# Seam of a hybrid layer kernel: feed forward's input sums reordered by product, first weight strip requested early, last block's residual rows written by accumulating transfers

## Chip, core and metric

One core of a Trainium2 chip runs the whole kernel. The metric is device time in microseconds (us) of one execution. All data are float32; TensorE works on pairs of float32r tiles ("hi" and "lo" parts), so that one product of full precision is three matmuls.

## Reference, cut to what matters

The layer works on `x` of 2048 tokens by 1024 channels. `chunked_gated_delta_rule`, the convolutions and the norms of the first half are left out here.

```python
h = adaln(x, g_norm_mix, shift_m, scale_m)
p = h @ w_in                       # 1024 -> 3592
...                                # convolutions, gated delta rule: ya, yb
y = concatenate([ya, yb]) @ w_out  # 1024 -> 1024
x = x + gate_m * y

h = adaln(x, g_norm_ffn, shift_f, scale_f)
gt, up = split(h @ w_gate_up, 2)   # 1024 -> 2 x 2816
x = x + gate_f * ((silu(gt) * up) @ w_down)
return adaln(x, g_norm_final, shift_o, scale_o)
```

## The kernel before, in words

The tokens are cut into 4 blocks of 512. The first half of the program (the mixing) takes them one after another: projections with `w_in`, convolutions, delta rule, and at the end of each block the out-projection with `w_out`. The second half (feed forward) first does gate and up with SiLU for 22 strips of 128 hidden channels, for two halves of the tokens, then the product with `w_down`. The seam is where the last block's out-projection ends and the first strip begins.

**Out-projection.** For block 3 it has two groups, one for each half of the output columns. A group is 4 weight pieces (`KPS`, order 0, 2, 3, 1) by 4 row tiles of 128 tokens, 24 matmuls a piece, and holds four PSUM banks of the pool `pd`, which has four. At its end each bank is read by VectorE (L1345, times `gate_m`) into a `cv` buffer (four of them); the old rows of `x` have been loaded into `cb` (L1343, two buffers), are added (L1346, by VectorE in the last block and by GpSimd in the others), and the sum is stored to the DRAM rows `x1d` (L1347). The second group can only start in a bank when VectorE has read it.

**Feed forward's sums.** Gate and up use a fast scheme of seven products in place of eight: `A11`, `A12`, `S2`, `S1`, `S3`, `S4`, `A22` on the token side (`SUMS`), and `B11`, `B21`, `T2`, `T1`, `T3`, `B22`, `T4` on the weight side. The token side is made from the normed, transposed input of blocks 0 and 1, which lies in DRAM as `xTd` (8 tiles of 128 x 512 per block). `first_sums` goes over `k` in 0 to 3; for each it loads four tiles, scales them on ScalarE (`load_scaled`, L603), and then makes all six sums' parts of this `k`: VectorE adds and subtracts (L623 to L629), and each result is split into hi (ScalarE cast, L598) and lo (VectorE subtract, L599) by `split_k`. So no sum is whole before the last `k`. `last_sum` makes `A22` after that. `run` walks one strip through the seven products in the order of `SUMS`.

**Weights of a strip.** `load_strips` loads a gate and an up piece of 512 KB (L384) into two of four `wraw` buffers. `prep_weights` then makes the weight sums with VectorE subtractions (L1389 to L1392) and splits them (`split_w`: ScalarE L389, VectorE L391). `T2` is one of the splits. In the seam the first strip is loaded and begun only after the mixing's program has ended.

**What sets the order.** Side work stands in generators, and `tick` runs a step of each after every 6 matmuls of the feed forward and every 3 of the mixing. A model of the chip, `Clock`, estimates when tiles are ready; up to the last block's `next_input` the order of each engine is pinned by its times, and after that it is the order of the program with what the framework's scheduler moves. Each engine works its own queue strictly in order. All loads and stores here are issued from SP's queue, in order too.

Of the kernel before, what the change touches and what calls it, by code (L numbers as in the profile page):

```python
# [20 lines left out]
P = 128  # L21
D = 1024
S = 2048
KD = D // P
# [186 lines left out]
def layer_kernel(ctx, tc, x, c, w_ada, b_ada, w_ada_final, b_ada_final, g_norm_mix, g_norm_ffn, g_norm_final,  # L211
# [105 lines left out]
    def drain():  # L317
        while side:
            tick(True)
# [86 lines left out]
    def out_groups(b):  # L406
        if b:
            return [[(n, kp, range(CH)) for kp in KPS] for n in range(2)]
        return [[(n, kp, range(2 * g, 2 * g + 2)) for kp in order for n in range(2)]
                for g, order in enumerate((KPS, sorted(KPS)))]  # L410

    def requests():
        for b in range(NB):
            for c0 in (2048, 1536, 2560, 3072):
                for h in range(NH):
                    yield col_strip, w_in, c0 + h * P
            for m in range(4):
                for c0 in (512, 1024, 0):
                    yield col_strip, w_in, c0 + m * P
            for g in out_groups(b):  # L420
                for n, kp, ts in g:
                    yield out_strip, n, kp
    reqs, ready, bg = requests(), deque(), deque()

    def fill(n):
# [177 lines left out]
        nc.scalar.activation(t, t, AF.Identity, scale=Gf[:, k:k + 1], bias=Sf[:, k:k + 1])  # L603


    def first_sums(A):
        pool = actx2.enter_context(tc.tile_pool(name="pA", bufs=1, side="right", reuse_waits="tile"))

        def tiles(n):
            return [pool.tile([P, 4, BLK], F32R, name=n + e) for e in ("h", "l")]  # L610

        for n in SUMS[:-1]:
            A[n] = tiles(n)
        for k in range(4):
            t = pool.tile([P, 4, BLK], F32, name="A22" + "hl"[k % 2])
            a, d, c_, e = (t[:, i, :] for i in range(4))
            for i, (b, kk) in enumerate(((0, k), (0, k + 4), (1, k), (1, k + 4))):
                load_scaled(t[:, i, :], b, kk)
            yield 1
            split_k(A["A11"], k, a)  # L620
            split_k(A["A12"], k, d)
            yield 1
            nc.vector.tensor_add(e, c_, e)  # L623
            nc.vector.tensor_sub(c_, a, c_)
            split_k(A["S1"], k, e)
            split_k(A["S3"], k, c_)
            yield 1
            nc.vector.tensor_sub(a, e, a)
            nc.vector.tensor_sub(d, d, a)  # L629
            split_k(A["S2"], k, a)  # L630
            split_k(A["S4"], k, d)
            yield 1
        A["A22"] = tiles("A22")

    def last_sum(A):
# [45 lines left out]
    with ExitStack() as actx:  # L681
# [144 lines left out]
        for b in range(NB):  # L826
# [482 lines left out]
            for g, group in enumerate(out_groups(b)):  # L1309
# [28 lines left out]
                for n, t in pso:  # L1338
                    ns = slice(n * 512, (n + 1) * 512)
                    row = b * CH + t  # L1340
                    take_now("cv", 1)
                    xr = ap_.tile([P, BLK], F32, name="cb", bufs=2)
                    nc.sync.dma_start(xr, x[row * P:(row + 1) * P, ns])  # L1343
# [34 lines left out]
                bg.popleft()  # L1378


    def prep_weights(raw, W):
# [3 lines left out]
        x = split_w(g, shape)  # L1385
# [84 lines left out]
    def run(hf, ms, refills):  # L1470
        W = [Ws.pop((hf, m)) for m in ms]
        a, s1, s2, s5, c_ = [], [], [], [], []
        for w in W:
            a.append(dense_ps())
            product(a[-1], w["B11"], A["A11"], True)
            s1.append(sg_tile())
            nc.scalar.copy(s1[-1], a[-1])
            work()
        if refills:
            refill(A, "A11")  # L1480
        for i, w in enumerate(W):
            b = misc_ps()
            product(b, w["B21"], A["A12"], True)
            nc.vector.tensor_add(s1[i], s1[i], b)
            nc.scalar.activation(s1[i], s1[i], AF.Silu)
            work()
        if refills:
            refill(A, "A12")
        for i, w in enumerate(W):
            product(a[i], w["T2"], A["S2"], False)  # L1490
            s2.append(sg_tile())
            nc.scalar.copy(s2[-1], a[i])
            work()
        if refills:
            refill(A, "S2")
        for i, w in enumerate(W):
            c_.append(misc_ps())
            product(c_[-1], w["T1"], A["S1"], True)
            s5.append(sg_tile())
            nc.scalar.copy(s5[-1], c_[-1])  # L1500
            work()
        if refills:
            refill(A, "S1")
        for i, w in enumerate(W):
            product(a[i], w["T3"], A["S3"], False)
            nc.vector.tensor_add(s5[i], s5[i], a[i])  # L1506
            work()
        if refills:
# [1 line left out]
            load_next()  # L1510
            prep_next()
        for i, w in enumerate(W):
            product(c_[i], w["B22"], A["S4"], False)
# [12 lines left out]
            work()  # L1526

        for i, w in enumerate(W):
            product(a[i], w["T4"], A["A22"], False)
            if (hf, ms[i]) == (1, NF - 1):  # L1530
                return lambda: tail(i)
            tail(i)
# [25 lines left out]
        jobs.append(steps())  # L1558

    strip_it, prep_it = iter(strips), iter(strips)  # L1560
    load_next()
    prep_next()
    work_off()
    load_next()
    spawn(last_sum(A), 1)
    spawn(second_half(), 8)
    for hf in range(2):
        m = 0
# [309 lines left out]
```

## Time and profile before

| | us |
|---|---|
| median of 3 runs (lowest, highest) | 2429.25 (2423.53, 2434.40) |
| the profiled execution, whole time | 2425.39 |
| its span, from first to last instruction | 2423.6 |
| PE busy in the span | 2350.6 (97%) |
| DVE, ACT, POOL busy | 1785.3, 1052.4, 564.9 |
| mean granted TensorE clock | 0.988 of full |

Each engine of the profile (PE is TensorE, DVE VectorE, ACT ScalarE, POOL GpSimd) has its own queue; "SPq" is the queue of SyncE, which issues transfers. A row of a timeline gives the start in us from the span's start, the duration, the engine, the source line, the operation, the tile written and those read, and in brackets how long the engine stood idle before it and what ended that. The next instruction of an engine may begin before the recorded end of the last, since they are pipelined: the cost of one in a run of equal ones is the distance of their starts.

### The profile page before, as it was taken

What the parts mean: (1) busy time and instruction counts of PE and PEld (TensorE: products, weight loads), DVE (VectorE), ACT (ScalarE), POOL (GpSimd) and SP (SyncE); (2) the same over time, 40 slices, a digit from 0 to 9 for tenths busy, and PEclk for the clock granted to TensorE, in tenths of its full rate; (3) what the DMA queues carried; (4) which work ended last, traced back from release to release, by engine and by line L of the source; (5) the groups of instructions that cost most, each with busy time, mean ns of one, the idle gap of its engine ahead of it and who ended that gap; (6) DMA issues with size and microseconds to landing.
All of it is one profiled execution on the core that took longest, in us unless ns stands there. A gap on an engine that the chain in (4) does not pass through costs nothing.

```text
span 2423.6 us, 30975 instructions
## 1 busy us (share of the span) xinstructions
PE 2350.6 (97%) x11285; PEld 1945.0 (80%) x11285; DVE 1785.3 (74%) x2675; ACT 1052.4 (43%) x1787; POOL 564.9 (23%) x638
## 2 busy tenths in 40 slices
PE   7999999999999999999999999999999999999997
PEld 6788888787788788877888888788888877887786
DVE  5998789786967688787666556875655668877887
ACT  4643664354544473356443334433333322322345
POOL 0331344034413261200000000000000036434448
PEclk9999999999999999999999999999999999999999
DMA  7443655535553445145664334753333364333343
GB/s 250 122 120 85 194 173 161 146 113 165 144 131 104 119 139 139 50 159 174 213 205 117 102 103 126 239 161 95 114 100 105 108 248 149 117 109 118 135 134 143
DMA packets 402015, 341.19 MB, mean 141 GB/s; under 512 B 39859, under 2 KB 343228, under 8 KB 401862
## 3 DMA queue, kind: packets, MB, share of 16 engines
q1 hardware_dynamic: 401606, 339.11, 45.7%
q8 instruction: 88, 1.44, 0.2%
q14 instruction: 65, 0.53, 0.1%
q10 hardware_dynamic: 256, 0.10, 0.0%
HBM read 265.74 MB, written 73.41 MB: 140 GB/s over the span
## 4 chain that ended last, share of the span: by engine, by line
PE 53%; DVE 7%; DMA 4%; ACT 3%; POOL 2%; issue 2%; SPq 0%; DVEq 0%; ACTq 0%; POOLq 0%
PE pd L322 32%; PE pm L322 17%; DMA y<-xT 1%; DVE acc L1746 1%; DVE wlo L391 1%; DMA ra<-act 1%; POOL wraw L1675 1%; DMA y<-in_w_ada_final_dram 1%; DMA A12d<-y 1%; ACT whi L389 1%; ACT y L603 0%; PE pm L1038 0%; DVE cv L1268 0%; PE pm L1144 0%; PE pm L1030 0%
## 5 line engine op out<-in xcount | busy, mean ns | idle before, releaser
L389 ACT CAST whi<-wraw 128x1024 fp32r<-128x1024 f32 x286 | 299.8, 1050 | 395.0 <-PE pd L322 172.3
L391 DVE TENSOR_TENSOR wlo<-wraw,whi 128x1024 fp32r<-128x1024 f32 x286 | 361.4, 1265 | 108.9 <-ACT whi L389 106.3
L322 PE MATMUL pd<-hTh,whi 128*128 128x512 f32 x888 | 362.2, 409 | 0.6 <-ACT hTh L558 0.6
L322 PE MATMUL pd<-hTh,wlo 128*128 128x512 f32 x888 | 348.3, 392 | 0.0
L322 PE MATMUL pd<-hTl,whi 128*128 128x512 f32 x888 | 348.1, 392 | 0.1
L322 PEld LDWEIGHTS pd<-hTh,wlo 128*128 128x128 f32 x888 | 167.6, 189 | 36.5
L322 PEld LDWEIGHTS pd<-hTh,whi 128*128 128x128 f32 x888 | 168.3, 190 | 33.5 <-ACT hTh L558 1.0
L322 PEld LDWEIGHTS pd<-hTl,whi 128*128 128x128 f32 x888 | 168.4, 190 | 32.0 <-DVE hTl L559 0.9
L1552 POOL TENSOR_TENSOR wraw<-wraw 128x1024 f32<-128x1024 f32 x2 | 4.9, 2474 | 779.7 <-DMA wraw<-in_w_down_dram 779.7
L1506 DVE TENSOR_TENSOR sg<-sg,pd 128x512 f32<-128x512 f32 x44 | 30.2, 686 | 169.5 <-PE pd L322 163.1
L1746 DVE TENSOR_TENSOR acc<-acc,pd 128x512 f32<-128x512 f32 x192 | 127.3, 678 | 29.7 <-PE pd L322 29.7
L1629 ACT CAST xh<-ra 128x640 fp32r<-128x640 f32 (+1 forms) x88 | 62.3, 719 | 188.0 <-PE pm L322 143.3
L1196 DVE SCALAR_TENSOR_TENSOR cv<-pd,pcb,cv 128x511 f32<-128x511 f32 (+2 forms) x173 | 129.3, 747 | 5.2
L1638 POOL TENSOR_TENSOR xl<-ra,xh 128x640 fp32r<-128x640 f32 (+1 forms) x40 | 67.4, 1686 | 164.6 <-ACT xh L1629 158.7
L1746 DVE TENSOR_TENSOR acc<-acc,pm 128x512 f32<-128x512 f32 x120 | 81.5, 680 | 18.5 <-PE pm L322 17.9
L322 PE MATMUL pd<-whi,ym 128*128 128x512 f32 x256 | 84.8, 396 | 0.0
L1675 POOL TENSOR_TENSOR wraw<-wraw 128x512 f32<-128x512 f32 x40 | 70.3, 1780 | 40.3 <-DMA wraw<-in_w_down_dram 36.8
L322 PE MATMUL pd<-S2h,whi 128*128 128x512 f32 x176 | 69.5, 395 | 5.0 <-ACT whi L389 5.0
L322 PE MATMUL pd<-A22h,whi 128*128 128x512 f32 x176 | 69.7, 396 | 4.1 <-DVE sg L1506 4.1
L322 PE MATMUL pd<-A22l,whi 128*128 128x512 f32 x176 | 69.2, 393 | 0.0
L322 PE MATMUL pd<-S2h,wlo 128*128 128x512 f32 x176 | 69.2, 393 | 0.0
L322 PE MATMUL pd<-A22h,wlo 128*128 128x512 f32 x176 | 69.2, 393 | 0.0
(465 smaller groups left out, 6210.9 us busy)
## 6 DMA issues: line engine op xcount, KB each, us to landing
wraw<-in_w_in_dram SPq DMA_DIRECT2D x112, 512.0 KB, 4.9
wraw<-in_w_gate_up_dram SPq DMA_DIRECT2D x88, 512.0 KB, 3.7
ra<-act SPq DMA_DIRECT2D x80, 448.0 KB, 3.6
wraw<-in_w_out_dram SPq DMA_DIRECT2D x40, 512.0 KB, 3.6
act<-S SPq DMA_DIRECT2D x80, 256.0 KB, 2.2
act<-act SPq DMA_DIRECT2D x68, 256.0 KB, 2.2
wraw<-in_w_ada_dram SPq DMA_DIRECT2D x32, 512.0 KB, 4.5
wraw<-in_w_down_dram SPq DMA_DIRECT2D x22, 512.0 KB, 4.5
```

The costliest lines, as they stand in the source:

```text
L322: mm(*args, **kw)
L389: nc.scalar.copy(hi, raw)
L391: (lo_engines.popleft() if lo_engines else nc.vector).tensor_sub(lo, raw, hi.bitcast(F32))
L1196: nc.vector.scalar_tensor_tensor(cv[:, n - t:], u[:, :BLK - n + t], taps[t], cv[:, n - t:], op0=ALU.mult, op1=ALU.add)
L1506: nc.vector.tensor_add(s5[i], s5[i], a[i])
L1552: nc.gpsimd.tensor_mul(r, r, first_w["gate"])
L1629: nc.scalar.copy(hi, raw[:, c0:c1, :])
L1638: eng.tensor_sub(lo, raw, hi.bitcast(F32))
L1675: nc.gpsimd.tensor_mul(r[:, hs], r[:, hs], gate_f[:, hs])
L1746: nc.vector.tensor_add(accs[s, u][:, ns], accs[s, u][:, ns], ps)
```

## The change

Four things change, all around the seam.

1. `first_sums` is written by sum, not by `k`. `A11` and `A12` (which need block 0 alone) are made for all four `k` first, then the additions and `S2`, then `S1`, `S3`, `S4`, and `A22`. The scaled inputs stay in buffers: `a` and `d` in the place of `A22`, `c_` and `e` in the place of `S4`. Each step tells `tick` a time at which to go on, worked out from `Clock` ("VectorE's pace"), in place of "after the next 6 matmuls". `summed(n)` lets a product go only when its sum has been written down in the program.
2. `strip_ahead` puts the first strip's two loads and the split of its gate piece at the end of the mixing's list of weight requests.
3. In the last block VectorE's addition of `x` goes, with its loads. The old rows of `x` are copied DRAM to DRAM into `x1d` when block 3 begins (four transfers of 512 KB on SP's queue), and the eight products are added to them by transfers with an accumulate operation, issued by GpSimd.
4. The `drain()` at the end of the last block goes.

```diff
+    def strip_ahead():
+        raw = [raw_w(w_gate_up[:, c0:c0 + P].rearrange("(k p) n -> p k n", p=P), [P, KD, P]) for c0 in (0, FF)]
+        return raw, split_w(raw[0], [P, KD, P])
...
+        yield strip_ahead,
...
-        for k in range(4):
-            t = pool.tile([P, 4, BLK], F32, name="A22" + "hl"[k % 2])
-            a, d, c_, e = (t[:, i, :] for i in range(4))
-            for i, (b, kk) in enumerate(((0, k), (0, k + 4), (1, k), (1, k + 4))):
-                load_scaled(t[:, i, :], b, kk)
-            yield 1
-            split_k(A["A11"], k, a)
-            split_k(A["A12"], k, d)
-            yield 1
...
+        def split(n, k, src):
+            split_k(A[n], k, src[:, k, :])
+            return clock.ready(A[n][1][:, k, :]) - 1.5
...
+        for k in range(4):
+            load(a, 0, k, k)
+            load(d, 0, k, k + 4)
+        yield 1
...
+        for k in range(4):
+            scale(a, k, k)
+            scale(d, k, k + 4)
+            split("A11", k, a)
+            load(c_, 1, k, k)
+            load(e, 1, k, k + 4)
+            yield split("A12", k, d)
+        have.update(("A11", "A12"))
+        for k in range(4):
+            scale(c_, k, k)
+            scale(e, k, k + 4)
+            ak, dk, ck_, ek = (t[:, k, :] for t in (a, d, c_, e))
+            nc.vector.tensor_add(ek, ck_, ek)
+            nc.vector.tensor_sub(ck_, ak, ck_)
+            yield clock.ready(ck_) - 1.5
+            nc.vector.tensor_sub(ak, ek, ak)
+            nc.vector.tensor_sub(dk, dk, ak)
+            yield split("S2", k, a)
+        have.add("S2")
+        for n, t in (("S1", e), ("S3", c_), ("S4", d)):
...
+            for k in range(4):
+                yield split(n, k, t)
+            have.add(n)
...
+    def summed(n):
+        while n not in have:
+            tick(True)
+        return A[n]
...
+            for t in range(CH if b + 1 == NB else 0):
+                nc.sync.dma_start(x1d[b * CH + t], x[(b * CH + t) * P:(b * CH + t + 1) * P, :])
...
                     nc.vector.tensor_mul(yo, pso[n, t], gate_m[:, ns])
-                    (nc.gpsimd if b + 1 < NB else nc.vector).tensor_add(yo, yo, xr)
-                    nc.sync.dma_start(x1d[row][:, ns], yo)
+                    if b + 1 < NB:
+                        nc.gpsimd.tensor_add(yo, yo, xr)
+                        nc.sync.dma_start(x1d[row][:, ns], yo)
+                    else:
+                        nc.gpsimd.dma_start(x1d[row][:, ns], yo, accum_op=ALU.add)
                     give("cv", 1)
-            drain()
+            if b + 1 < NB:
+                drain()
```

How the instructions stand, before and now, at the places that the prediction speaks of.

VectorE's queue at the first group's end. L599 (now L605) is the lo part of a sum, L1345 (now L1389) the read of a bank. Before:

```order
L624 TENSOR_TENSOR A22l<-A22l 128x512
L599 TENSOR_TENSOR S1l<-A22l,S1h 128x512
L628 TENSOR_TENSOR A22l<-A22l 128x512
L599 TENSOR_TENSOR S3l<-A22l,S3h 128x512
L629 TENSOR_TENSOR A22l<-A22l 128x512
L599 TENSOR_TENSOR S2l<-A22l,S2h 128x512
L1345 TENSOR_TENSOR cv<-pd,gate_m 128x512
L599 TENSOR_TENSOR S4l<-A22l,S4h 128x512
L1346 TENSOR_TENSOR cv<-cv,cb 128x512
L1345 TENSOR_TENSOR cv<-pd,gate_m 128x512 x2
```

Now:

```order
L605 TENSOR_TENSOR A11l<-A22h,A11h 128x512
L605 TENSOR_TENSOR A12l<-A22l,A12h 128x512
L1389 TENSOR_TENSOR cv<-pd,gate_m 128x512
L605 TENSOR_TENSOR A11l<-A22h,A11h 128x512
L605 TENSOR_TENSOR A12l<-A22l,A12h 128x512
L1389 TENSOR_TENSOR cv<-pd,gate_m 128x512
L391 TENSOR_TENSOR wlo<-wraw,whi 128x1024
L653 TENSOR_TENSOR S4h<-S4l,S4h 128x512
L1389 TENSOR_TENSOR cv<-pd,gate_m 128x512
```

The first read of a bank stood behind two `k` steps' worth of sums; it now stands behind the parts of `A11` and `A12` of three `k` steps, and the reads are spread among the sums.

TensorE's queue in the second group, now (with numbers, which tell the banks apart: `pd_9745`, `pd_9756`, `pd_9763` and `pd_9774` are the first to fourth; `whi_9565` is of the first piece, `whi_9613` of the next).

```order
L322 MATMUL pd_9763<-whi_9565,yal_7593 128x512
L322 MATMUL pd_9745<-whi_9613,ym_9121 128x512
L322 MATMUL pd_9745<-wlo_9615,ym_9121 128x512
L322 MATMUL pd_9745<-whi_9613,ym_9122 128x512
L322 MATMUL pd_9745<-whi_9613,ym_9121 128x512
L322 MATMUL pd_9745<-wlo_9615,ym_9121 128x512
L322 MATMUL pd_9745<-whi_9613,ym_9122 128x512
L322 MATMUL pd_9756<-whi_9613,ym_9194 128x512
L322 MATMUL pd_9756<-wlo_9615,ym_9194 128x512
L322 MATMUL pd_9774<-whi_9565,yah_7592 128x512
```

Before, the first piece's four tiles followed each other; now the fourth bank is first wanted behind 18 matmuls of the first piece and 8 of the next.

VectorE's queue from the second group's end to the weights of the first strip (L1437 to L1440 are the weight subtractions, the first `wlo` after them is the lo part of `T2`). Now:

```order
L605 TENSOR_TENSOR S3l<-S4l,S3h 128x512 x4
L1389 TENSOR_TENSOR cv<-pd,gate_m 128x512
L605 TENSOR_TENSOR S4l<-A22l,S4h 128x512
L1389 TENSOR_TENSOR cv<-pd,gate_m 128x512 x3
L1438 TENSOR_TENSOR wraw<-wraw 128x512
L605 TENSOR_TENSOR S4l<-A22l,S4h 128x512 x3
L1437 TENSOR_TENSOR T_9930<-wraw 128x512
L1437 TENSOR_TENSOR T_9995<-wraw 128x512
L1439 TENSOR_TENSOR wraw<-wraw 128x512
L1448 TENSOR_TENSOR t3l<-T_9930,t3h 128x512
L1440 TENSOR_TENSOR wraw<-wraw 128x512
L391 TENSOR_TENSOR wlo<-wraw,whi 128x1024
```

Before, four additions of `cb` stood among these reads, and the first strip's SiLU with its table load stood on ScalarE ahead of the cast of `T2`; now the cast of `T2` comes first.

SP's queue behind the sums' loads, now (`x_12` to `x_15` are the last block's rows `x1d`; the eight accumulating transfers into them stand on GpSimd's queue, with nothing between):

```order
L384 DMA wraw<-in_w_gate_up_dram 128x8x128 x4
L608 DMA y<-xT_129 128x512 x4
L583 DMA y<-x_12_119 128x1024
L384 DMA wraw<-in_w_gate_up_dram 128x8x128 x2
L583 DMA y<-x_13_120 128x1024
L583 DMA y<-x_14_121 128x1024
L384 DMA wraw<-in_w_gate_up_dram 128x8x128
```

The order of these rows is as before, but the loads of `x_12` to `x_15` now wait for transfers of GpSimd's queue, and strips' weights stand behind them. The 14 stores and loads of L1347 and L1343 that stood ahead of them are gone from SP.

## Rows read from the trace of the kernel before

**Rows 1.** Stretches, PE alone: length, busy us (count), granted clock, DMA share, GB/s
```profile
1080.00:1085.00 5.00, 4.45 (x11) 0.50 0.54 171
1115.00:1119.00 4.00, 3.80 (x8) 0.50 0.84 280
```

**Rows 2.** PE in order of time: start, us, instruction, [idle before]
```profile
1070.99 0.39 PE L322 MATMUL pd<-whi,yal 128*128 128x512 f32 x1
...
1075.07 0.39 PE L322 MATMUL pd<-whi,yal 128*128 128x512 f32 x1
1080.55 0.80 PE L322 MATMUL pd<-whi,yah 128*128 128x512 f32 x1 [5.09 <-DVE cv L1345]
...
1084.98 0.40 PE L322 MATMUL pd<-wlo,yah 128*128 128x512 f32 x1
...
1109.73 0.39 PE L322 MATMUL pm<-A12h,wlo 128*128 128x512 f32 x1
1115.15 0.79 PE L322 MATMUL pd<-S2h,whi 128*128 128x512 f32 x1 [5.04 <-ACT whi L389]
...
1119.13 0.40 PE L322 MATMUL pd<-S2h,wlo 128*128 128x512 f32 x1
```

**Rows 3.** DVE in order of time, same columns
```profile
1075.60 0.68 DVE L599 TENSOR_TENSOR A12l<-A22l,A12h 128x512 fp32r<-128x512 f32 x1
1076.20 0.68 DVE L624 TENSOR_TENSOR A22l<-A22l 128x512 f32<-128x512 f32 x1
...
1097.39 1.22 DVE L391 TENSOR_TENSOR wlo<-wraw,whi 128x1024 fp32r<-128x1024 f32 x1
1098.53 0.68 DVE L624 TENSOR_TENSOR A22l<-A22l 128x512 f32<-128x512 f32 x1
```

**Rows 4.** DVE by line, 1063 to 1111: count, busy us, mean ns, idle before
```profile
L1346 DVE TENSOR_TENSOR cv<-cv,cb 128x512 f32<-128x512 f32 x8 | 5.5, 688 | 4.9 <-DMA cb<-in_x_dram 4.8
```

**Rows 5.** ACT in order of time
```profile
1061.50 1.52 ACT L603 ACTIVATE A22h<-A22h,Sf,Gf 128x512 f32<-128x512 f32 x2 [1.27 <-DMA A22h<-xT]
1062.92 0.61 ACT L598 CAST A11h<-A22h 128x512 fp32r<-128x512 f32 x1
1063.43 0.81 ACT L603 ACTIVATE A22h<-A22h,Sf,Gf 128x512 f32<-128x512 f32 x1
...
1112.24 1.28 ACT L1485 ACT_TABLE_LOAD   x1
...
1114.08 1.98 ACT L389 CAST whi<-wraw 128x1024 fp32r<-128x1024 f32 x2
```

**Rows 6.** PE in order of time, two later stops
```profile
1575.50 0.50 PE L322 MATMUL pd<-A22h,whi 128*128 128x512 f32 x1 [2.45 <-DVE sg L1506]
...
2287.81 0.50 PE L322 MATMUL pd<-dh,xh 128*128 128x512 f32 x1 [1.59 <-DVE acc L1746]
```

**Rows 7.** Stretches behind those two stops, PE alone, columns as above
```profile
1575.50:1580.00 4.50, 4.50 (x13) 0.62 0.01 1
2287.80:2291.80 4.00, 3.99 (x17) 1.00 0.60 227
```

**Rows 8.** SyncE's issues and ACT in order of time, block 2's end
```profile
772.57 25.28 SPq L384 DMA_DIRECT2D wraw<-in_w_out_dram  x5
...
799.24 1.05 ACT L389 CAST whi<-wraw 128x1024 fp32r<-128x1024 f32 x1 [1.60 <-PE pd L322]
```

**Rows 9.** The page's list of issues: count, size, median us to landing
```profile
wraw<-in_w_in_dram SPq DMA_DIRECT2D x112, 512.0 KB, 4.9
...
act<-S SPq DMA_DIRECT2D x80, 256.0 KB, 2.2
```

**Rows 10.** SyncE's issues in order of time, seam
```profile
1113.30 0.43 SPq L577 DMA_DIRECT2D y<-x  x1
...
1129.61 3.27 SPq L384 DMA_DIRECT2D wraw<-in_w_gate_up_dram  x2
```

**Rows 11.** POOL in order of time
```profile
1123.34 0.48 POOL L524 TENSOR_SCALAR ss<-ss 128x1 f32<-128x1 f32 x1 [72.15 <-ACT ht L530]
```

More of the change, by code (lines that the diff above doesn't have):

```diff
@@ L603, in load_scaled, with tiles, load, scale @@
         nc.scalar.activation(t, t, AF.Identity, scale=Gf[:, k:k + 1], bias=Sf[:, k:k + 1])
+    have = set()
     def first_sums(A):
         pool = actx2.enter_context(tc.tile_pool(name="pA", bufs=1, side="right", reuse_waits="tile"))
-        def tiles(n):
-            return [pool.tile([P, 4, BLK], F32R, name=n + e) for e in ("h", "l")]
-        for n in SUMS[:-1]:
+        def tiles(n, dtype=F32R):
+            return [pool.tile([P, 4, BLK], dtype, name=n + e) for e in "hl"]
+        def load(t, b, k, k4):
+            nc.sync.dma_start(t[:, k, :], xTd[b][k4])
+        def scale(t, k, k4):
+            nc.scalar.activation(t[:, k, :], t[:, k, :], AF.Identity, scale=Gf[:, k4:k4 + 1], bias=Sf[:, k4:k4 + 1])
+        def split(n, k, src):
+            split_k(A[n], k, src[:, k, :])
+            return clock.ready(A[n][1][:, k, :]) - 1.5
+        a, d = tiles("A22", F32)
+        for n in ("A11", "A12"):
@@ L625, in first_sums @@
[L625 to L632, printed above, removed]
+            load(a, 0, k, k)
+            load(d, 0, k, k + 4)
+        yield 1
+        for n in ("S2", "S1", "S3"):
+            A[n] = tiles(n)
+        e, c_ = tiles("S4", F32)
+        for k in range(4):
[5 more added lines that the diff above has]
+            yield split("A12", k, d)
@@ new lines, in first_sums @@
+        have.update(("A11", "A12"))
[11 more added lines that the diff above has]
+        for n, t in (("S1", e), ("S3", c_), ("S4", d)):
+            if n == "S4":
+                A[n] = tiles(n)
+            for k in range(4):
+                yield split(n, k, t)
+            have.add(n)
@@ L633, in first_sums @@
         A["A22"] = tiles("A22")
+        yield from last_sum(A)
+        have.add("A22")
     def last_sum(A):
@@ L1341, in layer_kernel @@
                     take_now("cv", 1)
-                    xr = ap_.tile([P, BLK], F32, name="cb", bufs=2)
-                    nc.sync.dma_start(xr, x[row * P:(row + 1) * P, ns])
+                    if b + 1 < NB:
+                        xr = ap_.tile([P, BLK], F32, name="cb", bufs=2)
+                        nc.sync.dma_start(xr, x[row * P:(row + 1) * P, ns])
                     yo = cv_tile([P, 512])
                     nc.vector.tensor_mul(yo, pso[n, t], gate_m[:, ns])
-                    (nc.gpsimd if b + 1 < NB else nc.vector).tensor_add(yo, yo, xr)
-                    nc.sync.dma_start(x1d[row][:, ns], yo)
+                    if b + 1 < NB:
[3 more added lines that the diff above has]
+                        nc.gpsimd.dma_start(x1d[row][:, ns], yo, accum_op=ALU.add)
                     give("cv", 1)
-            drain()
+            if b + 1 < NB:
+                drain()
     bfin = b_ada_final.rearrange("(o n) -> o n", o=1)
@@ L1378, in bg_step, with prep_weights @@
                 bg.popleft()
-    def prep_weights(raw, W):
+    def prep_weights(raw, W, x=None):
         g, u = raw
@@ L1384, in prep_weights @@
         shape, half = [P, KD, P], [P, 4, P]
-        x = split_w(g, shape)
+        x = x or split_w(g, shape)
         W["B11"], W["B21"] = (*x, 0), (*x, 4)
@@ L1474, in run @@
             a.append(dense_ps())
-            product(a[-1], w["B11"], A["A11"], True)
+            product(a[-1], w["B11"], summed("A11"), True)
             s1.append(sg_tile())
@@ L1482, in run @@
             b = misc_ps()
-            product(b, w["B21"], A["A12"], True)
+            product(b, w["B21"], summed("A12"), True)
             nc.vector.tensor_add(s1[i], s1[i], b)
@@ L1489, in run @@
         for i, w in enumerate(W):
-            product(a[i], w["T2"], A["S2"], False)
+            product(a[i], w["T2"], summed("S2"), False)
             s2.append(sg_tile())
@@ L1497, in run @@
             c_.append(misc_ps())
-            product(c_[-1], w["T1"], A["S1"], True)
+            product(c_[-1], w["T1"], summed("S1"), True)
             s5.append(sg_tile())
@@ L1504, in run @@
         for i, w in enumerate(W):
-            product(a[i], w["T3"], A["S3"], False)
+            product(a[i], w["T3"], summed("S3"), False)
             nc.vector.tensor_add(s5[i], s5[i], a[i])
@@ L1512, in run @@
         for i, w in enumerate(W):
-            product(c_[i], w["B22"], A["S4"], False)
+            product(c_[i], w["B22"], summed("S4"), False)
             nc.vector.tensor_add(s2[i], s2[i], c_[i])
@@ L1528, in run @@
         for i, w in enumerate(W):
-            product(a[i], w["T4"], A["A22"], False)
+            product(a[i], w["T4"], summed("A22"), False)
             if (hf, ms[i]) == (1, NF - 1):
@@ L1560, in layer_kernel @@
     strip_it, prep_it = iter(strips), iter(strips)
-    load_next()
-    prep_next()
+    raw, x0 = ready.popleft()
+    s0 = next(strip_it), next(prep_it)
+    Ws[s0[0]] = {}
+    jobs.append(prep_weights(raw, Ws[s0[0]], x0))
     work_off()
     load_next()
-    spawn(last_sum(A), 1)
     spawn(second_half(), 8)
```

2 lines of the change are left out of this document (removed).

## Prediction

> **What bounds the kernel now.** I read the engines' shares first: TensorE is busy 97% of the span, so a change can save only what TensorE loses. Then I read TensorE in order of time across the seam, where every edit lies. Its rows there follow each other at 0.227 us (18 steps from 1070.99 to 1075.07 [rows 2]), the price P of one matmul. Two stops stand out. The first follows the product that began at 1075.07: the next began at 1080.55, so 5.48 - 0.23 = 5.25 us are lost, and the row names VectorE's read of a bank (L1345) as what ended the wait. The 10 products from 1080.55 to 1084.98 then took 4.43 instead of 10 x P = 2.27: 2.16 more. The granted clock of that stretch is 0.50, the lower of the two levels (1.2 GHz), after an engine that had stood idle for 5.09 us [rows 1, 2]. The second stop is alike: from 1109.73 to 1115.15, 5.19 lost, ended by ScalarE's cast of a weight sum, T2; then 8 products from 1115.15 to 1119.13 took 3.98 instead of 1.81, 2.17 more, at 0.50 again. Together 5.25 + 2.16 + 5.19 + 2.17 = **14.8 us**. That is the most the seam can give.
>
> Both stops are VectorE's. In the first its queue is full of sums: at 1075.60 and 1076.20 it still makes lo parts and subtractions [rows 3] while the banks wait. In the second, eight additions of the old `x` (8 x 0.60, the distance of two such starts [rows 3]) stood 4.9 us idle on their loads [rows 4] ahead of T2's subtraction, and a table load of 1.28 stood ahead of T2's cast at 1114.08 [rows 5].
>
> **The change, part by part.** *Sums by product.* The new order of VectorE's queue puts the first read of a bank behind three steps of `A11` and `A12` alone. I follow both engines from the last row that does not change. TensorE's first bank is complete at 1070.99 + 0.39 = 1071.4 [rows 2]; VectorE can read it then. The second group (96 matmuls), `A11` (12) and `A12` (12) follow each other if no bank comes late: 120 x P = 27.2, from 1075.3 to 1102.5. Up to the fourth bank's read VectorE has 14 instructions of 128x512 and one of 128x1024: 14 x 0.60 + 1.14 (1097.39 to 1098.53 [rows 3]) = 9.5, plus a wait of 0.35 (below): read at 1081.3. TensorE wants that bank behind 26 matmuls of the second group (three tiles of the first piece and eight matmuls of the next, by its new order), at 1075.3 + 5.9 = 1081.2: the first stop is gone, within 0.2 of a new one. The lost clock goes with it, since nothing stops TensorE ahead of it.
>
> *The end of the sums and T2.* From 1071.4 to the lo part of T2, VectorE's queue holds 48 instructions of 128x512 and 3 of 128x1024: 48 x 0.60 + 3 x 1.14 = 32.2. ScalarE, which makes the hi parts, has in front of these 10 scales (two in 1.42 from 1061.50), 9 casts (0.51 from 1062.92) and 2 weight casts (half of 1.98) [rows 5]: 7.1 + 4.6 + 2.0 = 13.7, from 1061.5 to 1075.2. VectorE's first addition wants the last of these scales behind 4 x 0.60 + 1.14, at 1074.9; with the signal between the engines I take 0.35. T2's lo part so begins at about 1104.0 and is there at 1105.2. T2's last subtraction is two instructions earlier, at about 1102.8, and its cast, now ahead of the table load, takes 1.0 more: the product `S2` begins at about 1104.0, not 1102.5. TensorE idles 1.6, makes two matmuls, and waits 0.85 for the lo part. **Left over: 2.45.**
>
> Does a stop of 1.6 bring the lower clock? The trace has stops of that order on both sides. The 1.59 at 2287.81 was followed by a stretch at 1.00, the 2.45 at 1575.50 by one at 0.62 [rows 6, 7]. 1.6 is nearest the first, so I take no loss; the bound is that 13 matmuls took 4.50 instead of 2.95, at most 1.6 more.
>
> *First strip split ahead.* What moves is the split of its gate piece, from behind the mixing to ahead of its end; its work is counted in the queues above. Its price is nothing otherwise: the two loads were SyncE's before too.
>
> *Additions removed.* Eight of VectorE's, 4.8 us of work and the 4.9 of waiting [rows 4]; both are already out of the 32.2. The loads and stores that leave SyncE cost TensorE nothing now, and their removal frees that queue.
>
> *Copies of x.* Four transfers of 512 KB stand on SyncE's queue at 772.57, ahead of weights whose cast follows at 799.24 [rows 8]. No row shows a copy from DRAM to DRAM. A load of 512 KB lands in 4.9, with other transfers in flight [rows 9]. Even one after another, four at 4.9 and the weights' own 4.9 make 24.5, within the 26.7 that are there. Free up to (26.7 - 4.9) / 4 = 5.4 each; I take nothing. Below nothing it can't be: it adds only.
>
> *Accumulating transfers.* Eight of 256 KB, on GpSimd's queue, which has no other work in the seam: its row at 1123.34 follows 72 us of nothing [rows 11]. The trace has none of this kind. The nearest: a plain store of 256 KB lands in 2.2, a 512 KB load, which moves as much as a read and a write of 256 KB, in 4.9 [rows 9]. Let each take p and all go in series. A bank's read needs one of four `cv` buffers; the eighth, at about 1098.2, needs the fourth transfer, begun after 1072: free up to p = (1098.2 - 1072) / 4 = 6.5. The load of the rows `x_14` stands on SyncE with strip weights behind it. Those were issued at 1129.61 [rows 10]; 12.3 earlier (the gain, below) is 1117, and I give the load 1 of it. It needs the seventh transfer: 1072 + 7p against 1116, so it costs 7p - 44, nothing up to about p = 6. Both near rows are under that: price nothing. The Trainium skill ("DMA: Bandwidth & Descriptors", section "Anatomy of one DMA — SWDGE (gpsimd) path") gives for a transfer issued by GpSimd 2.0 us and the bytes at 436 GB/s, which makes an estimate of 2.6 for 256 KB, an accumulate not named; by it the sum would be the same. No run shows it yet.
>
> **The sum.** 14.8 - 2.45 = **12.3 us gained**. Against the profiled execution that is 2425.4 - 12.3 = 2413.1. That execution lies 3.9 under the median of the three runs; against the median it is 2417.0. I take the middle, **2415**. (Below, a case's time is 2427.3 less its gain.)
>
> **Rivals.**
> - *The seam keeps more.* T2's cast or the fourth bank comes a little later than I add up: my margins there are 0.2 us in 10 and my left-over hangs on VectorE's queue of 51 instructions. With one stop as now (5.19 + 2.17 kept) the gain is 7.4: **2419.9**. With my 1.6 idle and a lower clock it is 10.7: 2416.6. For it: VectorE has no idle time in the whole stretch, so each late hi part shifts all. Against: ScalarE has less to do than VectorE there. Chance 0.22.
> - *All of it goes.* VectorE's 0.35 does not occur and its instructions start closer than 0.60: gain 14.8, **2412.5**. Against: 1.6 us are not found in a row of 51. Chance 0.10.
> - *Slower: accumulating transfers in series, about 10 us each.* A read, an addition and a write, behind SyncE's weight loads, could take twice the slowest near row. Then the eighth bank's read waits (1072 + 40 = 1112), and `x_14` and the strip weights behind it wait 7 x 10 - 44 = 26: net 13.7 lost, **2441**. It decides from 7p - 44 = 12.3, p = 8.0. Against: both near rows are far under. For: DMA engines are already 84% busy in the second stop [rows 1], and VectorE works without a gap as those transfers are issued. The Trainium skill ("SBUF — State Buffer", section "SBUF: two separate sides") has a rule that would make it so: descriptors of transfers issued by GpSimd are written by GpSimd's cores, which VectorE locks out while it runs a two-port mode. VectorE's rows of the seam are all two-input operations [rows 3, 4], for which the same page (section "Who interferes with whom") names no such mode, so I give it little. Chance 0.07.
> - *The change doesn't do what it says:* the model's clock, by which sums are let go, puts them elsewhere on the chip's time; but the order is fixed in the program and was read from it, so only TensorE's place against it can differ. That is the first rival, not a further one.
>
> Mine: 0.61.
>
> **How the numbers follow.** What a measurement of this kernel can tell from no change is about 0.5%, 12.1 us: faster means under 2417.1. My case, 2415, lies 2 us inside, and its base is uncertain by 3.9, so I split its 0.61 as 0.36 faster and 0.25 same; the full gain is faster (0.10), the first rival same (0.22, of which 0.02 faster when the runs come out low). The slow one is slower, 0.07. That makes 0.48 faster, 0.45 same, 0.07 slower. Range: from 2407, the full gain against the lowest run (2423.5 - 14.8 = 2408.7) less a little, to 2428, where transfers cost all the gain (p = 8), between the base 2427.3 and the median. Only the slow rival, and runs that are spread wider than those three, lie outside.
>
> **What would show it.** In the profile after: TensorE without a gap from 1071 to about 1102, the granted clock at 1.00 throughout; a stop of 1 to 2 us ahead of the first `S2` product, ended by ScalarE's cast, and a small one for the lo part. VectorE without idle time on loads. GpSimd's transfers landing in 2 to 6 us each. Four copies at about 773 with no new wait of TensorE behind them. I would be wrong by the step "fourth bank" if TensorE stops within the second group, by "T2" if it stops longer than 2.5 at `S2`, by "accumulating transfers" if a later bank read waits for a `cv` buffer or a strip's weights come late after 1105, by "copies" if anything changes between 775 and 1060.

## The result, and the profile after

| us | before | after |
|---|---|---|
| median of 6 runs (lowest, highest) | 2426.26 (2421.96, 2434.40) | 2413.97 (2408.69, 2416.30) |
| span of the profiled execution | 2423.6 | 2406.9 |
| mean granted TensorE clock | 0.988 | 0.994 |

The ratio of the runs is 0.9942, with a 95% interval of 0.9929 to 0.9955: 14 us faster by the ratio, 12.3 by the medians. The change was timed a second time beside two experiments (below): 2412.50 against 2422.93, ratio 0.9959 (0.9944 to 0.9973).

The two profiled spans differ by 16.7 us, more than the medians do. To see where, I compared the two traces matmul by matmul: both programs issue 11285 of them, and the last product of a projection (tile `hTh`), some 1047 us behind the first matmul, comes before anything in the seam. The execution after reached it 3.2 us sooner, that of the second timing 0.3 sooner; on the way, where both programs issue the same matmuls in the same order, the first lead moves between 0.5 and 3.3 us from the first 100 us on. I put that part down to scatter. From that product on, TensorE's lead in the seam is 12.9 us in the one and 12.5 in the other. Behind the seam the two part again: at the last matmul the leads from that product on are 14.0 and 7.3 us, in two executions of one program. The table at the end of the experiments has it for every kernel.

TensorE in order of time after the change: the last matmul that completes the first bank of group 1, then the end of product `A12` and the start of `S2`.

```profile
1067.95 0.39 PE L322 MATMUL pd<-whi,yal 128*128 128x512 f32 x1
...
1099.67 0.39 PE L322 MATMUL pm<-A12h,wlo 128*128 128x512 f32 x1
1101.07 0.50 PE L322 MATMUL pd<-S2h,whi 128*128 128x512 f32 x1 [1.01 <-ACT whi L389]
1101.40 0.40 PE L322 MATMUL pd<-S2l,whi 128*128 128x512 f32 x1
1102.33 0.50 PE L322 MATMUL pd<-S2h,wlo 128*128 128x512 f32 x1 [0.53 <-DVE wlo L391]
```

The first answers to the row at 1070.99 before [rows 2]. Between these two ends no row tells of a stop: the one of 5.09 us is gone. Where 5.04 us stood ahead of `S2` there are 1.01, ended by the cast of T2, and 0.53 for its lo part. The lower clock of the two stretches before (0.50 [rows 1]) is gone too. The stretch up to `S2` and that from `S2` on, TensorE alone: length, busy time (count), granted clock, DMA share, GB/s.

```profile
1070.00:1101.00 31.00, 29.95 (x131) 1.00 0.60 121
1101.07:1105.00 3.93, 3.40 (x14) 1.00 1.09 291
```

VectorE in order of time: the first read of a bank and the instruction behind it, the fourth read, and the lo part of T2.

```profile
1068.38 0.69 DVE L1389 TENSOR_TENSOR cv<-pd,gate_m 128x512 f32<-128x512 f32 x1 [0.25 <-PE pd L322]
1069.29 0.69 DVE L605 TENSOR_TENSOR A11l<-A22h,A11h 128x512 fp32r<-128x512 f32 x1 [0.22 <-ACT A11h L604]
...
1077.68 0.68 DVE L1389 TENSOR_TENSOR cv<-pd,gate_m 128x512 f32<-128x512 f32 x1
...
1101.05 1.23 DVE L391 TENSOR_TENSOR wlo<-wraw,whi 128x1024 fp32r<-128x1024 f32 x1
```

GpSimd in order of time: its issues of the accumulating transfers (a row with x2 holds two).

```profile
1069.40 1.09 POOL L1394 DMA_DIRECT2D x<-cv  x1 [21.29 <-DVE cv L1389]
1071.49 0.88 POOL L1394 DMA_DIRECT2D x<-cv  x1 [1.00 <-DVE cv L1389]
1073.81 0.86 POOL L1394 DMA_DIRECT2D x<-cv  x1 [1.43 <-DVE cv L1389]
1078.72 0.88 POOL L1394 DMA_DIRECT2D x<-cv  x1 [4.05 <-DVE cv L1389]
1093.68 0.87 POOL L1394 DMA_DIRECT2D x<-cv  x1 [14.08 <-DVE cv L1389]
1094.88 1.74 POOL L1394 DMA_DIRECT2D x<-cv  x2 [0.33 <-DVE cv L1389]
1098.86 0.88 POOL L1394 DMA_DIRECT2D x<-cv  x1 [2.24 <-DVE T L1437]
```

From issue to landing, shortest, median and longest of the eight, and then of the fifth alone, from the view of that source line:

```profile
DMA to landing us min/median/max: 3.7/6.4/8.6
DMA to landing us min/median/max: 4.9/4.9/4.9
```

The transfers take 3.7 to 8.6 us, more than the stores (2.2) and most of them more than the loads (4.9) [rows 9]. TensorE's two waits in the seam name none of them. What comes nearest is a strip's weights that reach VectorE late, behind a load of rows of `x` on SyncE's queue; VectorE's row, then SyncE's issue of these weights:

```profile
1109.71 0.69 DVE L1437 TENSOR_TENSOR T<-wraw 128x512 f32<-128x512 f32 x1 [1.91 <-DMA wraw<-in_w_gate_up_dram]
```

```profile
1102.31 2.12 SPq L384 DMA_DIRECT2D wraw<-in_w_gate_up_dram  x2
```

The load ahead of them waited 2.3 us for a transfer and was issued at 1098.60. The weights followed only at 1102.31, when VectorE had made the lo part of T2 (1101.05 + 1.23 = 1102.28), whose end that issue waited for. So the transfers did not make them late. TensorE loses nothing by it: its lead is 12.3 us at n = 240 of the table and 12.9 at n = 400.

### The profile page after: what moved, and what is told of

It reads as the page before. It is cut to its first block, busy times and chain, and to the rows that moved or that the text cites. A ratio compares the mean times of both kernels' runs of the same rounds, so it can differ in the third digit from the quotient of the medians.

```text
span 2406.9 us, 30953 instructions
## 1 busy us (share of the span) xinstructions
PE 2341.2 (97%) x11285; PEld 1936.8 (80%) x11285; DVE 1780.5 (74%) x2667; ACT 1050.9 (44%) x1787; POOL 574.9 (24%) x646
## 4 chain that ended last, share of the span: by engine, by line
PE 73%; DVE 12%; DMA 4%; ACT 4%; issue 3%; POOL 2%; SPq 0%; ACTq 0%; DVEq 0%; POOLq 0%
PE pd L322 47%; PE pm L322 18%; DVE wlo L391 2%; DVE acc L1795 1%; DMA wraw<-in_w_in_dram 1%; DVE cv L1239 1%; ACT whi L389 1%; DMA y<-xT 1%; DVE wraw L469 1%; PE pm L906 1%; PE pm L1081 1%; DVE cv L1311 1%; POOL wraw L1724 1%; DVE cv L1237 1%; PE pm L1073 0%
## 5 line engine op out<-in xcount | busy, mean ns | idle before, releaser
L322 PE MATMUL pm<-S4h,whi 128*128 128x512 f32 x176 | 68.6, 390 | 1.4 <-ACT sg L1548 1.4
L322 PE MATMUL pd<-S3h,t3h 128*128 128x512 f32 x176 | 69.1, 393 | 0.0
```

The lines of the kernel that those rows point to most:

```text
L322: mm(*args, **kw)
```

## Experiments

In each, the edit is to the changed kernel if nothing else is said.

**Sums k by k again.** `first_sums` as before; `have` is filled at its end.

```diff
-        for k in range(4):
-            scale(a, k, k)
-            scale(d, k, k + 4)
-            split("A11", k, a)
...
+        for n in SUMS[:-1]:
+            A[n] = tiles(n)
+        for k in range(4):
+            t = pool.tile([P, 4, BLK], F32, name="A22" + "hl"[k % 2])
...
+        have.update(SUMS[:-1])
```

> The change with its sums again written k by k (first strip still split ahead, transfers still accumulating). I measure each trace by TensorE's time from the last projection product (hTh) to the first S1 product: 67.2 us before, 54.9 after the change. My theory (the order of the sums removes the first stop, the other edits the second): the first stop is back, about 5 us and 2 of lost clock, the second is under 1: 54.9 - 1.9 + 7.4, so 60 to 61 us, a ratio to the kernel before of about 0.997. Rival (VectorE is relieved by the additions alone, the order is nothing): 55 to 57 us, ratio 0.994 to 0.995.

Measured: 61.0 us from `hTh` to `S1`; ratio 0.9990 (0.9979 to 1.0001). TensorE in order of time, its three stops:

```profile
1078.49 0.80 PE L322 MATMUL pd<-whi,yah 128*128 128x512 f32 x1 [5.29 <-DVE cv L1366]
...
1110.42 0.50 PE L322 MATMUL pd<-S2h,whi 128*128 128x512 f32 x1 [1.56 <-ACT whi L389]
1111.63 0.52 PE L322 MATMUL pm<-S1h,whi 128*128 128x512 f32 x1 [0.47 <-ACT whi L389]
```

The first stop is back whole, by the same read of a bank. The second, which I had expected under 1 us, has shrunk from 5.0 to 1.6 and 0.5. So the order of the sums is what removes the first stop, and the other edits act on the second. The ratio is worse than I expected, though the 61.0 lies in my range: that measure ends at `S1`, and this program has moved other matmuls behind it. Counted by matmuls (the table) the lead is 2.3 us. Behind the 1.56 and 0.47 the clock also came down, which I had not put into the sum:

```profile
1110.42:1114.00 3.58, 3.11 (x8) 0.72 0.90 197
```

**Additions on VectorE again.** Loads and stores of L1343 and L1347 as before, no copies, no accumulating transfers.

```diff
-                        nc.gpsimd.dma_start(x1d[row][:, ns], yo, accum_op=ALU.add)
+                        nc.vector.tensor_add(yo, yo, xr)
+                        nc.sync.dma_start(x1d[row][:, ns], yo)
```

> The change without the accumulating transfers and the copies: the last block's rows are loaded and added by VectorE again. My theory: eight additions of 0.60 and some waits on their loads, 5 to 8 us, stand on VectorE ahead of T2, so the stop at S2 grows from 1.0 to 6 to 9 us and the low clock is back behind it (2 us): 61 to 65 us from hTh to S1, ratio 0.997 to 0.999. Rival (the first stop was the one that counted and the additions fit beside the rest): 55 to 57 us, ratio 0.994 to 0.995.

Measured: 63.1 us, within what I expected; ratio 0.9998 (0.9989 to 1.0006), a little worse. TensorE's two stops, and the row of ScalarE that bears on the second:

```profile
1111.15 0.79 PE L322 MATMUL pd<-S2h,whi 128*128 128x512 f32 x1 [7.85 <-ACT whi L389]
...
1131.50 0.50 PE L322 MATMUL pd<-A22h,whi 128*128 128x512 f32 x1 [3.03 <-ACT A22h L604]
```

```profile
1127.00 1.52 ACT L609 ACTIVATE y<-y,Sf,Gf 128x512 f32<-128x512 f32 x2 [3.77 <-DMA y<-xT]
```

The first stop stays away, and the stop at `S2` is larger than before the change. A further 3.03 us come at `A22`: its cast stands on ScalarE behind a scale that waited 3.77 us for a load of `xT`. In the change the four loads of that kind were issued together at 1094; here two of them stand on SyncE's queue behind three strip weights, at 1122. So this edit undoes more than the additions. ScalarE's order changed with it, too: T2's subtraction was done at 1108.8, but its cast began only at 1110.07, behind the table load at 1108.24, which is up to 1.3 of the 7.85. With all this back, the new order of the sums and the early split bring nothing in the end; the time of the first stop has moved to later ones.

**Additions on GpSimd.** As in the other blocks, in place of copies and transfers.

```diff
-                        nc.gpsimd.dma_start(x1d[row][:, ns], yo, accum_op=ALU.add)
+                        nc.gpsimd.tensor_add(yo, yo, xr)
+                        nc.sync.dma_start(x1d[row][:, ns], yo)
```

> The change with the last block's additions on GpSimd, as in the other blocks (loads, GpSimd addition, store), in place of copies and accumulating transfers. My theory (what counts is that VectorE doesn't add; the accumulating transfers bring nothing of their own): S2 waits 0 to 2 us longer since loads and stores are on SyncE's queue again, 55 to 57.5 us, ratio 0.994 to 0.996. Rival (the transfers themselves, or SyncE's queue free of 14 issues, carry the gain): over 60 us, ratio 0.997 or more.

Measured: 65.0 us; ratio 1.0003 (0.9994 to 1.0012). My theory fell here: to rid VectorE of the additions is not enough. GpSimd in order of time, then VectorE in the same stretch, then two of TensorE's stops:

```profile
1072.37 1.30 POOL L1387 TENSOR_TENSOR cv<-cv,cb 128x512 f32<-128x512 f32 x1 [21.08 <-ACT A22l L625]
1075.55 2.16 POOL L1387 TENSOR_TENSOR cv<-cv,cb 128x512 f32<-128x512 f32 x1 [1.89 <-ACT S4h L625]
1078.95 1.67 POOL L1387 TENSOR_TENSOR cv<-cv,cb 128x512 f32<-128x512 f32 x1 [1.23 <-DVE cv L1386]
```

```profile
1068.49 0.69 DVE L605 TENSOR_TENSOR A12l<-A22l,A12h 128x512 fp32r<-128x512 f32 x1
...
1072.63 1.58 DVE L605 TENSOR_TENSOR A11l<-A22h,A11h 128x512 fp32r<-128x512 f32 x1 [0.39 <-ACT A11h L604]
...
1076.47 1.79 DVE L653 TENSOR_TENSOR S4h<-S4l,S4h 128x512 f32<-128x512 f32 x1
...
1079.39 1.78 DVE L653 TENSOR_TENSOR S4h<-S4l,S4h 128x512 f32<-128x512 f32 x1
```

```profile
1084.84 0.80 PE L322 MATMUL pd<-whi,yah 128*128 128x512 f32 x1 [2.44 <-DVE cv L1386]
...
1111.33 0.50 PE L322 MATMUL pd<-S2h,whi 128*128 128x512 f32 x1 [3.27 <-ACT whi L389]
```

VectorE's instruction of two SBUF inputs takes 0.69 at 1068.49, with GpSimd idle, and 1.58, 1.79 and 1.78 where GpSimd adds. The Trainium skill states this ("SBUF — State Buffer", section "Who interferes with whom"): a VectorE instruction with two SBUF inputs contends with a GpSimd instruction that reads SBUF. The rows agree: each of the three slow instructions ends 0.54 or 0.55 us behind the end of the addition on GpSimd that it ran beside. Bank reads come late by it. The fourth is 12.55 us behind the first (1084.10 - 1071.55), in the change 9.30, and the three slow instructions between them make 3.1 of that difference. VectorE's waits in this stretch name no load and no store, so the other half of my rival, SyncE's fuller queue, is not what held the banks; how much of the stop at `S2` it has is not shown. As issuer of transfers GpSimd leaves VectorE alone: in the trace after, VectorE's sums take 0.68 or 0.69 through all eight issues.

**First strip split behind the mixing again.**

```diff
-        yield strip_ahead,
...
-    raw, x0 = ready.popleft()
-    jobs.append(prep_weights(raw, Ws[s0[0]], x0))
+    load_next()
+    prep_next()
```

> The change without the first strip's split ahead. My theory, in which VectorE's queue has as many instructions either way: its lo part comes 1 to 1.5 us late at A11, and the stop at S2 is smaller by about that: 55 to 57 us, ratio 0.994 to 0.996. Rival (the early split is what makes the seam close): A11 and A12 wait several us with a lower clock behind, 59 to 63 us, ratio 0.996 to 0.998.

Measured: 53.9 us, under my 55, but `S1` comes ten matmuls earlier in this program, so the table is the better measure; ratio 0.9959 (0.9945 to 0.9973), as expected. TensorE's stops (one of 0.39 at `S2`, at 1107.61, is left out):

```profile
1102.35 0.50 PE L322 MATMUL pd<-A11h,wlo 128*128 128x512 f32 x1 [1.01 <-DVE wlo L391]
...
1109.26 0.50 PE L322 MATMUL pm<-S1h,whi 128*128 128x512 f32 x1 [0.92 <-ACT whi L389]
...
1131.00 0.66 PE L588 MATMUL pm<-ck,y 128*128 128x128 f32 x4 [1.45 <-ACT y L583]
```

The stops at `A11`, `S2` and `S1` together are 2.3 us, the change's two 1.5. Then 1.45 us more wait for the transposes' input (L588), as I take it since work was pushed back; no run shows that by itself. By matmuls the early split is worth about 3 us at n = 400, half of it already at n = 240; in whole times the two kernels can't be told apart.

**One part alone, on the kernel before.** The order of the sums alone, and copies with accumulating transfers alone.

> The kernel before with the sums by product alone (VectorE adds x, the first strip is split behind the mixing, the drain is back). My theory (each edit alone only moves the wait): the first stop goes (7 us), but A22's parts, the additions and the strip's split now stand together on VectorE ahead of A11's third matmul or of S2: a stop of 7 to 11 us there with a lower clock behind, 65 to 69 us from hTh to S1, ratio 0.998 to 1.001. Rival (the order of the sums is worth its 7 us alone): 59 to 61 us, ratio 0.996 to 0.9975.

> The kernel before with copies and accumulating transfers alone (sums k by k, no early split, the drain is kept). My theory: the first stop stays (7.4 us), the second shrinks to under 2 us since VectorE is rid of 4.8 us of additions and 4.9 of waiting: 60 to 62 us from hTh to S1, ratio 0.997 to 0.999. Rival (the second stop is ScalarE's table load and casts, not VectorE's additions): 65 to 68 us, ratio 0.999 to 1.0.

Measured: the order alone 65.0 us, ratio 0.9983 (0.9974 to 0.9991); the transfers alone 61.8 us, ratio 0.9974 (0.9962 to 0.9985), both as expected. TensorE's stop with the order alone, ended by the lo part of the first strip's weights:

```profile
1109.08 0.79 PE L322 MATMUL pd<-A11h,wlo 128*128 128x512 f32 x1 [9.83 <-DVE wlo L391]
```

and its two with the transfers alone:

```profile
1080.47 0.79 PE L322 MATMUL pd<-whi,yah 128*128 128x512 f32 x1 [5.29 <-DVE cv L1348]
...
1111.95 0.50 PE L322 MATMUL pd<-S2h,wlo 128*128 128x512 f32 x1 [0.53 <-DVE wlo L391]
```

Each edit removes one stop; the order alone builds a new one of 9.83 us, in `A11`, ahead of the place of the old second. By matmuls (n = 400) they lead by 2.7 and 5.2 us, together (the kernel without the early split) by 9.7, with the split by 12.9 and 12.5. So by this lead the two edits are worth 1.8 us more together than their sum of 7.9. Two things limit that: the kernel with both has lost the `drain()` as well, which no run tried by itself, and the whole times don't show it (0.0017 and 0.0026 of the time apart, 0.0041 together, each uncertain by about 0.001). That all of them draw on the one queue of VectorE would explain it; it is argued, not shown.

**Slower transfers.** Each accumulating transfer issued twice, and four times.

> The change with each accumulating transfer issued twice (the second waits for the first; the products of the last block are so added twice). In the trace after the change a transfer lands 3.7 to 8.6 us behind its issue, but three are under way at a time. My theory: the first group's are through before the second group's banks are read, the second group's end some 8 us later, and the weights behind the load of x_12 on SyncE come about 5 us late: 2 to 8 us more than the change, from hTh to S1 55 to 59 us, ratio 0.996 to 0.998. Rival, the formula of my slow case with 2 x 6.4 us each in series (7p - 44): 45 us more, ratio over 1.01.

> The same with each transfer issued four times (the products of the last block are so added four times). My theory: now the first group's transfers are still under way when the second group's banks are read, and the load of x_12 waits 15 to 25 us with a strip's weights behind it: a stop of 10 to 20 us in the first or second strip, ratio 1.000 to 1.005. Rival (SyncE's queue has slack and the transfers are hidden in any number): ratio under 0.998.

Measured: twice 59.0 us, ratio 0.9978 (0.9969 to 0.9988); four times 71.0 us, ratio 1.0096 (1.0082 to 1.0110). Three of TensorE's stops, twice:

```profile
1106.45 0.50 PE L322 MATMUL pd<-S2h,whi 128*128 128x512 f32 x1 [2.53 <-ACT whi L389]
...
1108.31 0.50 PE L322 MATMUL pd<-S2h,wlo 128*128 128x512 f32 x1 [1.13 <-DVE wlo L391]
...
1124.17 0.50 PE L322 MATMUL pd<-A22h,whi 128*128 128x512 f32 x1 [3.55 <-DVE sg L1555]
```

and four times, with two lines of VectorE's waits there (total, times, longest):

```profile
1119.04 0.79 PE L322 MATMUL pd<-S2h,whi 128*128 128x512 f32 x1 [15.85 <-ACT whi L389]
...
1142.89 0.80 PE L322 MATMUL pm<-S4h,whi 128*128 128x512 f32 x1 [13.56 <-ACT sg L1551]
```

```profile
DVE T L1440 <- DMA wraw<-in_w_gate_up_dram: 20.3, 1, 20.3
DVE cv L1389 <- DMA x<-cv: 10.6, 2, 5.4
```

Doubled, the transfers take back 5 to 9 us of the gain by the ratios (0.9978 against 0.9942 and 0.9959), about the top of what I expected; four times they take back all of it and 23 us more, beyond what I expected. The mechanism is the one that I priced: a strip's weights come 20.3 us late behind the load of a row of `x` that waits for its transfers, and bank reads wait 10.6 for `cv`. The formula 7p - 44 is not: with 2 x 6.4 it gives over 45 us. Up to three transfers are under way together, so the fourfold 32 landed within 68 us of each other, one in 2.2, not one in 6.

**What is given back.** The lead of 12.9 falls to 10.8 in the fifth strip (the fourth, as I had counted). TensorE's two stops there, and the rows of VectorE and ScalarE that stand ahead of what they wait for:

```profile
1191.73 0.50 PE L322 MATMUL pm<-S4h,whi 128*128 128x512 f32 x1 [1.42 <-ACT sg L1548]
1195.85 0.50 PE L322 MATMUL pd<-A22h,whi 128*128 128x512 f32 x1 [1.08 <-DVE sg L1554]
```

```profile
1194.51 0.69 DVE L712 TENSOR_TENSOR y<-y 128x512 f32<-128x512 f32 x1 [4.67 <-DMA A12d<-y]
```

```profile
1190.40 0.81 ACT L609 ACTIVATE y<-y,Sf,Gf 128x512 f32<-128x512 f32 x1 [1.28 <-DMA y<-xT]
```

Both rows are the second half's sums, which wait for stores and loads of their own. I began this work later:

```diff
-    spawn(second_half(), 8)
+    spawn(second_half(), 14)
```

> The change with the second half's sums (second_half) begun after 14 in place of 8 steps of side work. In the trace after the change two stops, 1.42 and 1.08 us in the fourth strip, stand behind ScalarE's scales and VectorE's sums that wait for this half's loads and stores; the trace before has one of 0.69 there. Theory: they are a part of the seam's gain given back, since TensorE now comes earlier to work whose transfers did not move; begun later, that work no longer stands ahead of the strip's own: 2 to 4 us less than the change, ratio 0.992 to 0.994. Rival: the same waits come one or two strips later, ratio as the change, 0.994 to 0.995.

> The same begun after 28 steps. Theory: the same 2 to 4 us less than the change, ratio 0.992 to 0.994; no more, since the two stops are gone already at 14. Rival: the second half's sums now come late for the stores that later strips read: ratio 0.995 or more.

> The change itself, beside the two others on the same chip: ratio 0.993 to 0.9955, from hTh to S1 54 to 56 us, and the first 1047 us of the program within 3 us of before either way (the start of the profiled execution was 3 us faster than before's; if that comes from the change and not from scatter, it is 3 us faster again).

Measured: 14 steps 2413.70 us, ratio 0.9960 (0.9947 to 0.9974); 28 steps 2414.91, 0.9965 (0.9952 to 0.9978); the change itself 2412.50, 0.9959 (0.9944 to 0.9973). My theory of 2 to 4 us fell, and the rival holds: the two stops are gone, and others come later. Lines of TensorE's waits from 1060 to 1400 us (total, times, longest), 14 steps and 28:

```profile
PE pd L322 <- ACT sg L1540: 4.3, 3, 2.2
```

```profile
PE pd L322 <- ACT sg L1540: 1.8, 2, 1.4
PE pd L322 <- DVE sg L1554: 1.4, 1, 1.4
```

No version was found that beats the change.

**TensorE's lead over the kernel before**, in us, at the nth matmul behind the last projection product (minus is ahead; worked out from the start times in the traces; the first stop of before lies ahead of n = 130, the second between 200 and 240):

```
n                              130    240    400    700   1000
the change                    -7.0  -12.3  -12.9  -10.8  -10.8
the change again              -6.7  -12.0  -12.5  -10.3   -9.0
sums k by k                   +1.0   -2.2   -2.3   -0.7   -0.5
additions on VectorE          -7.2   -4.1   +0.2   +2.5   +1.9
additions on GpSimd           -2.8   -1.7   +2.1   +4.3   +3.2
split behind the mixing       -6.8  -10.9   -9.7   -7.8   -7.0
order of the sums alone       -7.0   -2.2   -2.7   -1.9   -2.4
transfers alone               +0.9   -5.4   -5.2   -2.8   -1.7
transfers twice               -6.6   -8.2   -1.1   -2.1   -2.9
transfers four times          -6.8   +3.8  +23.8  +24.1  +24.3
second half after 14 steps    -6.7  -12.0  -11.7  -10.2   -7.7
second half after 28 steps    -7.0  -12.2  -11.1  -13.8  -10.7
```

## Why the prediction was right

- *The time.* 2415 was forecast, with 2407 to 2428 around it, and 2413.97 and 2412.50 were measured. The gain in the seam was put at 12.3 us; the traces have 12.3 and 12.0 at n = 240. That the whole time came out as near is in part luck: some 2 us and more are given back behind the seam, which the sum does not have, single runs spread over 8 us, and the times alone could not tell my case from *all of it goes* (2412.5). The traces tell them apart.
- *Fourth bank.* Put within 0.2 us of a new stop, and it is at that edge. In the trace after, the product that first wants this bank began 0.50 behind the one before it (1077.92 to 1078.42), not 0.23. In the second timing TensorE stopped:

```profile
1081.44 0.50 PE L322 MATMUL pd<-whi,yah 128*128 128x512 f32 x1 [0.45 <-DVE cv L1389]
```

  By my own words a stop within the second group says that this step is wrong. It is off by these 0.3 to 0.6 us, and the gain ahead of it (7.0 and 6.7 at n = 130) stays.
- *T2.* I had 32.6 us from the first bank's end to T2's lo part; the rows have 1101.05 - 1068.34 = 32.7. TensorE came to the end of `A12` 0.4 later than I had it (1099.67 + 0.23 - 1067.95 = 31.95 for my 31.5), so it idled 1.0 and not 1.6. The left-over by starts is 1101.07 - 1099.67 - 0.23 = 1.17 and 1102.33 - 1101.40 - 0.23 = 0.70, together 1.87 for my 2.45. My own times give 2.25: the lo part at 1105.2 against 1102.5 and two matmuls. The 0.1 in 33 is luck in one term: the wait of 0.35 that I put ahead of VectorE's first addition is not there (it starts at 1072.23 without idle time); a wait of nearly that size comes a little earlier, at 1069.29, for ScalarE's cast of a part of `A11`.
- *Clock.* That a stop of this order costs no clock held here (1.00). My reason for it, the stop's length beside two rows, did not: 1.56 us (with 0.47 close behind) in the kernel with sums k by k were followed by 0.72, and 3.55 with transfers twice by 1.00.
- *Additions removed.* I took VectorE's 4.8 us and 4.9 of waiting as all there was. The step that makes VectorE's queue fit is right (its undoing takes the whole gain). What I did not see is that its undoing also changes the order of SyncE's loads and ScalarE's casts: 3.03 us at `A22` and up to 1.3 at `S2` come with that.
- *Copies of x.* Between 690 and 1024 us of the program the lead in the trace after stays within 0.4 us: nothing, as forecast, though a copy is slower than I had allowed in series (7.7 us to landing in the view of its line, for 5.4).
- *Accumulating transfers.* Hidden, as forecast, but for another reason than the one that I gave: each is slower than I took it (3.7 to 8.6, not 2 to 6, nor the estimate of 2.6), and they go up to three at a time, not in series. The formula of the slow rival so put the point from which they cost at p = 6 to 8; with each transfer doubled, the whole is still faster than before, and only with four it is slower. The sign that I had named, a strip's weights late after 1105, is there by its wording (1.91 us of VectorE at 1109.71), but the transfers are not its cause and TensorE lost nothing by it.
- *The first rival* (one stop stays) is what the transfers alone give (5.2 us of lead at n = 400, for my 7.4); the order alone gives less, with its new stop of 9.83; *the second* (all of it goes) missed by the 1.9 us left over.
- What I had not looked at is the fifth strip, where some 2 us of the gain are given back.

## What to carry to other kernels

Where two stops hang on one engine's full queue, follow that queue by count of instructions from the last row that stays as it is; here it met the chip to 0.1 us in 33, if with some luck in one term. Don't price the parts of such a change one by one without looking at what comes next: the order alone made a new stop nearly as long as the old two together. Of the three places that were tried for the additions, transfers did best; given to GpSimd as arithmetic on SBUF the work came back as slower VectorE instructions.

## What the runs showed of the hardware

- GpSimd's queue held three of these 256 KB accumulating transfers. The eighth issue, at 1098.86, came after 2.24 us of idling, though VectorE had read the last bank by 1095.7 (the row names a VectorE instruction, `T`, that this transfer does not read). It began 0.3 us behind the landing of the fifth (1093.68 + 4.9), with the sixth and seventh under way. In the traces of the sums k by k, of the late split and of the second timing the fourth of a run of issues likewise began 0.25 to 0.32 us behind the landing of the first. What sets the limit was not tried.
- VectorE's two-input instructions take 1.58 to 1.79 us in place of 0.69 while GpSimd adds from SBUF (above).
- The length of a stop alone doesn't tell whether the lower clock follows. The stretch behind 3.55 us, transfers twice:

```profile
1124.17:1128.00 3.83, 3.83 (x21) 1.00 0.82 260
```
